# Up projection: half of the transposes of six column groups go from TensorE to SyncE's DMA queue, by way of two-byte planes

## The chip, the cores and the metric

The kernel runs on one core of a Trainium2 chip. The core has five engines with instruction streams of their own: TensorE (PE in the profile; PEld is its loading of weights), VectorE (DVE), ScalarE (ACT), GpSimd (POOL) and SyncE (SP). The data lie in SBUF, 128 partitions; products come out in PSUM; DMA queues, issued by SyncE, ScalarE and GpSimd, move data between SBUF and DRAM, and within SBUF.

The metric is the device time of one execution in microseconds, smaller is better. Before the change it was 1339.47 us, the median of three runs from 1339.23 to 1339.55. The profiled execution took 1339.37 us.

## What is computed

The reference is one encoder layer in float32: 256 tokens, width 2048. Two attention branches are gated, projected and added to the residual stream; then comes the part that the change touches, a squared-ReLU perceptron of inner width 8192:

```python
h = rms_norm(x, norm_mlp_pre[l])
u = jnp.square(jax.nn.relu(jnp.einsum('bsd,df->bsf', h, w_up[l])))
x = x + rms_norm(jnp.einsum('bsf,fd->bsd', u, w_down[l]), norm_mlp_post[l])
```

## The kernel before

Every product is made in split precision: each float32 operand is cut into a high part (a cast by ScalarE) and a low part (a subtraction on VectorE), and three products, high by high, high by low and low by high, are added in PSUM. Some blocks of a product are made with seven block products in place of eight. For those, VectorE makes sums of the weights (`u_0t`, `u_3t`, `u_5t`), which are split in turn (`u_0eh`, `u_0el` and so on).

The up projection has eight groups (`g` from 0 to 7), each of 1024 of the 8192 columns. A group has eight steps, one for each 256 rows of `w_up`; in most groups the order of the rows is 1, 2, 0, 4, 3, 6, 5, 7, and rows 0, 3 and 5 go by seven products. The raw weights of a step (1 MB) are loaded by SyncE into one of three buffers (`u_3r` is the raw tile of rows 3), and split into `u_3h` and `u_3l`. `Weights.next` (L710) asks for the weights of two steps ahead: at step `n` it traces the load and the split of position `n + 2`, each instruction of it ordered behind the instruction kept in `uw.behind` where the two are on the same engine. `u_piece` (L1183) adds the last partial result at the end of a group, sets `uw.behind` to that addition on VectorE, and lets ScalarE apply ReLU with the row's scale.

The result `z` of a group has tokens along the partitions: for each of two token blocks, two halves of 512 columns. The down projection needs it the other way around, so each half is transposed during the next group. `u_T` (L1165) does it: eight 128x128 transposes on TensorE (L1170) into two PSUM banks (`uT`), and a Square of each bank by ScalarE into a page `u` (L1173). It is called at the steps 1 and 2 of the group behind, for the first and the second half. `u_sets` then calls `act_sets`, which splits `u` into high and low parts (`ah`, `al`) and lets GpSimd store them in DRAM (`keeph`, `keepl`); for the first half, of even number, it also makes the sums `sm`. That happens at steps 3 and 5. The last group transposes both of its predecessor's halves at steps 1 and 2 and stores at 1 and 2, and the last group's own halves are transposed in the down projection.

A planner orders the instructions of each engine while the program is built: what is ready in its own model of time goes first, and among several, what was written first. On the chip each engine then runs its list in order, and SyncE starts its DMAs in order too. The pages of 4 KB a partition come from one pool of 27.

Of the kernel before, what the change touches and what calls it, by code (L numbers as in the profile page):

```python
# [10 lines left out]

F32 = mybir.dt.float32
F32R = mybir.dt.float32r
AF = mybir.ActivationFunctionType
ALU = mybir.AluOpType
AX = mybir.AxisListType

P = 128
D = 2048
T = 256  # L20
KD = D // P
DFF = 4 * D
# [28 lines left out]
def encoder_layer(ctx: ExitStack, tc: tile.TileContext, a, out):  # L51
    nc = tc.nc
# [12 lines left out]
    def page(shape, dt, name):  # L65
        return pages.tile(shape, dt, tag="pg", name=name)
# [4 lines left out]
    def t2k(name, dt=F32):  # L71
        return tmp.tile([P, 2, T], dt, tag="t2k", name=name, bufs=7)
# [6 lines left out]
    def small(w, name):  # L79
        return tiny.tile([P, w], F32, tag=f"s{w}", name=name)  # L80
# [37 lines left out]
    def split(raw, name, pieces=2, after=(), then=None):  # L118
# [3 lines left out]
        _, nk, cw = (P, len(raw), 512) if listed else raw.shape  # L122
        hi = wp.tile([P, nk, cw], F32R, tag="hi", name=f"{name}_h")
        lo = wp.tile([P, nk, cw], F32R, tag="lo", name=f"{name}_l")
        prev = front if then else ()
# [172 lines left out]

    hT = [page([P, 2, 512], F32R, f"hT{i}") for i in range(8)]

    def x_part(k):
# [3 lines left out]
        g = g_pre[:, k : k + 1]  # L305
        i = nc.scalar.activation(d[:, :T], src, AF.Copy, scale=g).ins
        j = nc.vector.scalar_tensor_tensor(  # L307
# [30 lines left out]
    def x_squares(i):  # L338
        for t in range(2):
            j = junk512("jx0").rearrange("p a b -> p (a b)")  # L340
            nc.scalar.activation(
                j, xp[i][:, t], AF.Square, accum_out=ssx[:, t * 4 + i : t * 4 + i + 1]
            )
# [10 lines left out]
    def head_constants():  # L354
# [5 lines left out]
        le = small(2, "le")  # L360
        nc.scalar.activation(le, ls, AF.Exp)
        nc.vector.scalar_tensor_tensor(
# [55 lines left out]
    def parts(dst, at, src):  # L418
        hi, lo = dst
        nc.scalar.copy(hi[at], src)  # L420
        nc.vector.tensor_sub(lo[at], src, hi[at].bitcast(F32))
# [34 lines left out]
    def v_evac(dst):  # L456
        hi, lo = dst

        def evac(t, ps):
            r = rx[:, t : t + 1]  # L460
            nc.scalar.activation(hi[:, t], ps, AF.Copy, scale=r)
            nc.vector.scalar_tensor_tensor(
# [5 lines left out]
    def p_transposed(p, name):  # L468

        pt = bank(f"{name}_pt")  # L470
        for kt in range(2):
            for t in range(2):
# [4 lines left out]
                )  # L477
        r = [t2k(f"{name}_pT{i}", F32R) for i in range(2)]
        parts(r, slice(None), pt.rearrange("p (k q) -> p k q", k=2))
        return r  # L480

    def diff_head(h, qT, kT, v, hl, sc):
        p = t2k(f"dp{h}")
        for t in range(2):
# [19 lines left out]
            for c in range(2):  # L504
                nc.scalar.activation(
                    e[:, c],
                    s[:, c * T : (c + 1) * T],
                    AF.Exp,
                    bias=nbs[:, c : c + 1],
# [27 lines left out]
        for t in range(2):  # L537
            nc.scalar.activation(
                on[:, t], o[:, t * T : (t + 1) * T], AF.Square, accum_out=ss[:, t : t + 1]
            )  # L540
# [5 lines left out]
        for eb in range(2):  # L546
            for t in range(2):
# [4 lines left out]
                )  # L552
        ot = page([P, 2, 512], F32R, f"oaT{h}")
        for eb in range(2):
# [8 lines left out]
    def na_head(h, qT, kT, v, hl):  # L563
# [47 lines left out]
        if h % 2 == 0:  # L611
            oT["nt", h // 2] = page([P, 2, 512], F32R, f"onT{h}")
        ot = oT["nt", h // 2][:, h % 2]
# [49 lines left out]
    def pair_weights(view, name, seven, low=None, after=None, paged=False):  # L663
# [32 lines left out]
            nc.vector.tensor_sub(l2[i], t[i], h2[i].bitcast(F32))  # L696
        return h1, l1, h2, l2

    class Weights:


# [73 lines left out]
    def wide_group(name, kinds, weights, stat7, stat8, mm_banks, z, piece, each=None, turn=None, after={}, in_order=False):  # L775

        any7 = any(s for _, s in kinds)
        pr = Products(name, mm_banks)  # L780
        pr.in_order = in_order
        for n, (i, seven) in enumerate(kinds):
            w = weights.next(after)
            if each:
                each(n)
            if seven:
                final = not any(s for _, s in kinds[n + 1 :])
                pr.seven(partial(stat7, i), w, final)
                if final:
                    pr.combine(z)  # L790
                continue
            end = n == len(kinds) - 1
            if turn and n < 2:
                ahead = [*ahead, (i, w)] if n else [(i, w)]
                for t in range(2) if n else ():
                    for ii, ww in ahead:
                        for which in (2 * t, 2 * t + 1):
                            pr.eight(partial(stat8, ii), ww, which, False)
                    if not t:
                        turn()  # L800
                continue
            for which in range(4):
                pr.eight(partial(stat8, i), w, which, end)
                if end:
                    b, t, half = PLAIN[which]
                    piece(t, half, pr.ps[b], any7)

    def sums_of(p1, p2, name):

        a11, a21, a12, a22 = p1[:, :P], p1[:, P:], p2[:, :P], p2[:, P:]  # L810
        s = page([P, 4, P], F32, f"{name}s")
        nc.vector.tensor_sub(s[:, 0], a21, a22)
        nc.vector.tensor_sub(s[:, 1], a11, a21)
        nc.vector.tensor_sub(s[:, 2], s[:, 0], a11)
        nc.vector.tensor_add(s[:, 3], a12, s[:, 2])
        parts_ = page([P, 2, 4, P], F32R, name)
        nc.scalar.copy(parts_[:, 0], s)
        nc.vector.tensor_sub(parts_[:, 1], s, parts_[:, 0].bitcast(F32))
        return parts_
# [77 lines left out]
    for h in range(2):  # L897
        gate = []
        for br, gc, src, o in (("a", GA, a["w_branch_a"], "a"), ("b", GB, a["w_branch_b"], "n")):
            z = [page([P, 2, 512], F32, f"g{br}{h}{t}") for t in range(2)]  # L900
# [183 lines left out]
    def first_up(n):  # L1084
        for t, c in {2: [(1, 1), (0, 2)], 3: [(1, 2), (0, 3)], 4: [(1, 3)]}.get(n, ()):
            residual_parts(t, c)
        if n == 5:
            for t in range(2):
                mlp_squares(t)
                mlp_scale(t)  # L1090
            for i in range(4):
                kd = dram.tile([P, 1024], F32, name=f"keepx{i}", tag=f"keepx{i}")
                nc.gpsimd.dma_start(kd, x2[i])
                kept["x", i] = kd
# [67 lines left out]
    def u_T(cg, z):  # L1162

        u = page([P, 4, T], F32, f"u{cg}")
        for b in range(2):  # L1165
            pt = bank(f"uT{cg}{b}")
            for j in range(2):
                for t in range(2):
                    c = (b * 2 + j) * P
                    nc.tensor.transpose(  # L1170
                        pt[:, j * T + t * P : j * T + (t + 1) * P], z[t][:, cg % 2, c : c + P], ident
                    )
            nc.scalar.activation(  # L1173
                u[:, b * 2 : b * 2 + 2], pt.rearrange("p (j q) -> p j q", j=2), AF.Square
            )
        return u

    def u_sets(cg, u):

        got = act_sets(cg, u)  # L1180
        if NG - 4 <= cg < NG - 2:
            sets[0, cg] = got
# [11 lines left out]
    def ups(g):  # L1194
        return ALL8 if g == 0 else LAST_UPS if g == DFF // 1024 - 1 else UPS

    uw = Weights()
# [19 lines left out]
                uw.ask(wd[:, :, cg, j, g * 1024 : (g + 1) * 1024], f"d{g}{cg}{j}", seven, page)  # L1217
    uz = None
    us = {}
    for g in range(DFF // 1024):  # L1220
        z = Late(lambda g=g: [page([P, 2, 512], F32, f"u{g}{t}") for t in range(2)])

        def up_each(n, g=g, uz=uz):
            if not g:
                first_up(n)
                if n == 7:
                    for i in (0, 3, 5):
                        f = page([P, 2, T], F32, f"h2f{i}")
                        for k in range(2):
                            d = hT2[i][:, k].bitcast(F32)  # L1230
                            nc.vector.tensor_add(f[:, k], d[:, :T], d[:, T:])
                        h2sum[i] = sums_of(f[:, 0], f[:, 1], f"h2s{i}")
                return
            cg = g * 2 - 3 + n
            if n in (1, 2):
                us[cg] = u_T(cg, uz)
            steps = (3, 5) if g < DFF // 1024 - 1 else (1, 2)
            if n in steps:
                cg = g * 2 - 2 + steps.index(n)
                u_sets(cg, us[cg])  # L1240

        wide_group(
            f"u{g}",
            ups(g),
            uw,
            h2stat7,
            h2stat8,
            (1, 2, 3, 7),
            z,
            partial(u_piece, z=z),  # L1250
            each=up_each,
            turn=None if g else turn_rows,
            after={} if g else {2: scaled[0]},
        )
        uz = z
# [133 lines left out]
    for g in range(2):  # L1389
        pr = Products(f"p{g}", (1, 2, 3, 7))  # L1390
        pr.in_order = True
        for bi, b in enumerate(blocks[g]):
            end = bi == len(blocks[g]) - 1
            for n, (cg, j, seven) in enumerate(down_steps(g, bi)):
# [42 lines left out]
                for which in range(4):  # L1437
# [4 lines left out]
                    if last:  # L1442
                        bank_, t, half = PLAIN[which]
# [65 lines left out]
```

## Time and profile before

| | us |
|---|---|
| median of three runs | 1339.47 |
| the profiled execution, its own time | 1339.37 |
| its span in the profile | 1337.6 |
| ScalarE busy | 740.3 |
| one up group, from start to start | 43.3 |
| transposes of the up projection, in number (16 blocks of 8) | 128 |

The span is the time from the first to the last instruction on the core; the execution's own time is a little longer. A row of a group of instructions names the line, the engine, the operation, what is written and read, and its count and time. A row of the timeline begins with its start in us from the start of the span and its length; in brackets stands the idle time of the engine before it and what ended it. A matmul's length covers its whole passage through the array, so neighbours overlap; the distance of the starts is what one costs. In a list of waits the engine that waits stands first, then what it waited for, the sum, the number and the longest.

### The profile page before, as it was taken

What the parts mean: (1) busy time and instruction counts of PE and PEld (TensorE: products, weight loads), DVE (VectorE), ACT (ScalarE), POOL (GpSimd) and SP (SyncE); (2) the same over time, 40 slices, a digit from 0 to 9 for tenths busy, and PEclk for the clock granted to TensorE, in tenths of its full rate; (3) what the DMA queues carried; (4) which work ended last, traced back from release to release, by engine and by line L of the source; (5) the groups of instructions that cost most, each with busy time, mean ns of one, the idle gap of its engine ahead of it and who ended that gap; (6) DMA issues with size and microseconds to landing.
All of it is one profiled execution on the core that took longest, in us unless ns stands there. A gap on an engine that the chain in (4) does not pass through costs nothing.

```text
span 1337.6 us, 16286 instructions
## 1 busy us (share of the span) xinstructions
PE 1329.0 (99%) x6305; PEld 1113.4 (83%) x6305; DVE 1096.8 (82%) x1277; ACT 740.3 (55%) x869; POOL 39.4 (3%) x73
## 2 busy tenths in 40 slices
PE   9999999999999999999999999999999999999997
PEld 8888888888888888888888888888888888888886
DVE  7978766667787897885688999999988988898886
ACT  6655554544545555555476666666555555555542
POOL 0000000000000000000100000000000000000000
PEclk9999999999999999999999999999999999999999
DMA  9874655564564656567658677877797998798995
GB/s 354 277 215 161 193 168 176 184 187 157 189 220 172 207 190 207 188 232 254 226 184 277 239 253 273 297 239 245 250 360 287 402 379 311 271 372 330 358 351 207
DMA packets 114125, 335.85 MB, mean 251 GB/s; under 512 B 16768, under 2 KB 17280, under 8 KB 114048
## 3 DMA queue, kind: packets, MB, share of 16 engines
q1 hardware_dynamic: 94368, 265.87, 57.5%
q10 hardware_dynamic: 12960, 43.26, 8.4%
q0 software_dynamic: 6720, 25.69, 4.9%
q8 instruction: 49, 0.80, 0.2%
q14 instruction: 28, 0.23, 0.0%
HBM read 307.01 MB, written 29.61 MB: 252 GB/s over the span
## 4 chain that ended last, share of the span: by engine, by line
PE 75%; issue 21%; DMA 1%; DVE 1%; ACT 1%; POOL 0%; SPq 0%; POOLq 0%; ACTq 0%
PE u L742 25%; PE ga L742 6%; PE gb L742 6%; PE ba L742 3%; PE bb L742 3%; PE y L742 3%; PE qn_p L223 2%; PE ka_p L223 2%; PE kn_p L223 2%; PE qa_p L223 2%; PE ka_p L225 1%; PE qn_p L225 1%; PE kn_p L225 1%; PE vn_p L267 1%; PE vn_p L266 1%
## 5 line engine op out<-in xcount | busy, mean ns | idle before, releaser
L223 PE MATMUL qn_p<-hT,qn_h 128*128 128x512 f32 x128 | 45.9, 400 | 0.0
L223 PE MATMUL kn_p<-hT,kn_h 128*128 128x512 f32 x128 | 45.6, 400 | 0.0
L223 PE MATMUL ka_p<-hT,ka_h 128*128 128x512 f32 x128 | 45.2, 399 | 0.0
L742 PE MATMUL u<-u_2h,h2T 128*128 128x512 f32 x128 | 44.0, 396 | 0.0
L223 PE MATMUL qa_p<-hT,qa_h 128*128 128x512 f32 x128 | 43.6, 399 | 0.3 <-DVE hT L307 0.3
L742 PE MATMUL u<-u_1h,h2T 128*128 128x512 f32 x128 | 43.4, 389 | 0.0
L742 PE MATMUL u<-u_4h,h2T 128*128 128x512 f32 x128 | 43.2, 391 | 0.0
L742 PE MATMUL u<-u_7h,h2T 128*128 128x512 f32 x128 | 41.0, 389 | 0.0
L742 PE MATMUL u<-u_6h,h2T 128*128 128x512 f32 x128 | 41.0, 389 | 0.0
L225 PE MATMUL qn_p<-hT,qn_l 128*128 128x256 f32 x128 | 35.9, 281 | 0.0
L225 PE MATMUL kn_p<-hT,kn_l 128*128 128x256 f32 x128 | 35.7, 280 | 0.0
L225 PE MATMUL ka_p<-hT,ka_l 128*128 128x256 f32 x128 | 35.2, 282 | 0.0
L225 PE MATMUL qa_p<-hT,qa_l 128*128 128x256 f32 x128 | 32.5, 282 | 0.1
L145 DVE TENSOR_TENSOR y_l<-y_w,y_h 128x1024 fp32r<-128x1024 f32 x16 | 19.0, 1222 | 11.9 <-ACT y_h L137 11.9
L223 PEld LDWEIGHTS kn_p<-hT,kn_h 128*128 128x128 f32 x128 | 24.0, 188 | 5.4
L223 PEld LDWEIGHTS qn_p<-hT,qn_h 128*128 128x128 f32 x128 | 24.1, 188 | 5.3
L145 DVE TENSOR_TENSOR kn_l<-kn_w,kn_h 128x1024 fp32r<-128x1024 f32 x16 | 19.0, 1220 | 11.5 <-ACT kn_h L137 11.5
L223 PEld LDWEIGHTS ka_p<-hT,ka_h 128*128 128x128 f32 x128 | 23.9, 188 | 5.3
L742 PEld LDWEIGHTS u<-u_1h,h2T 128*128 128x128 f32 x128 | 24.0, 188 | 5.0
L145 DVE TENSOR_TENSOR vn_l<-vn_w,vn_h 128x1024 fp32r<-128x1024 f32 x16 | 19.0, 1221 | 11.2 <-ACT vn_h L137 11.2
L742 PEld LDWEIGHTS u<-u_7h,h2T 128*128 128x128 f32 x128 | 24.0, 188 | 5.0
L742 PEld LDWEIGHTS u<-u_6h,h2T 128*128 128x128 f32 x128 | 24.0, 188 | 5.0
(1632 smaller groups left out, 4567.5 us busy)
## 6 DMA issues: line engine op xcount, KB each, us to landing
bh<-keeph ACTq DMA_DIRECT2D x30, 512.0 KB, 9.1
bl<-keepl ACTq DMA_DIRECT2D x30, 512.0 KB, 10.6
keeph<-ah POOLq DMA_DIRECT2D x18, 512.0 KB, 3.8
keepl<-al POOLq DMA_DIRECT2D x18, 512.0 KB, 7.1
va_w<-in_w_in SPq DMA_DIRECT2D x8, 1024.0 KB, 5.2
qn_w<-in_w_in SPq DMA_DIRECT2D x8, 1024.0 KB, 5.2
kn_w<-in_w_in SPq DMA_DIRECT2D x8, 1024.0 KB, 5.1
vn_w<-in_w_in SPq DMA_DIRECT2D x8, 1024.0 KB, 5.0
```

Of the source, the lines that this page charges most:

```text
L145: sub = nc.vector.tensor_sub(lo[part], src, hi[part].bitcast(F32)).ins
L223: nc.tensor.matmul(ps[b], hi[:, k % 4, cs], mv, start=(k == 0), stop=False)
L225: nc.tensor.matmul(ps[b][:, :T], lo[:, k % 4, cs], mv[:, :T], start=False, stop=(k == nk - 1))
L266: nc.tensor.matmul(ps[t], sh, hi[:, k % 4], start=(k == 0), stop=False)
L267: nc.tensor.matmul(ps[t], sh, lo[:, k % 4], start=False, stop=False)
L742: ins = nc.tensor.matmul(self.ps[i], st, mv[:, blk], start=i not in self.begun, stop=last and n == 2).ins
```

## The change

For the groups 1 to 6 (`by_dma`), the second half of the previous group's columns no longer goes through `u_T`. At step 1, ahead of the first half's `u_T`, `sent` splits each float32 into its two 16-bit halves: ScalarE copies, for each token block, 512 numbers a partition, read as 1024 two-byte elements at a stride, into two planes (low and high halves). One DMA from SyncE's queue then transposes the 128 x 2048 two-byte elements into a page `got`, 16 blocks of 128 x 128. At step 3, `joined` lets ScalarE copy the 2048 elements a partition back, interleaved, into a page `u`, and a Square over the whole page follows in place. The storing at steps 3 and 5 stays. `uw.behind` is set to the transposing DMA, so the loads that are traced from step 2 of the group on, those of position 4 and after, follow it in SyncE's queue. Group 7 and the down projection keep TensorE's transposes for both halves.

```diff
+    def sent(z, name):
+
+        planes = page([P, 2, 2, 512], U16, f"{name}_s")
+        for t in range(2):
+            nc.scalar.copy(planes[:, t], z[t].bitcast(U16).rearrange("p (c h) -> p h c", h=2))
+        got = page([P, 16, P], U16, f"{name}_g")
+        moved = nc.sync.dma_start(got, planes.rearrange("p t h c -> p (t h c)"), transpose=True)
+        return got, moved.ins
+
+    def joined(got, dst):
+
+        nc.scalar.copy(
+            dst.rearrange("p k q -> p (k q)")
+            .bitcast(U16)
+            .rearrange("p (k t q h) -> p t h k q", k=4, t=2, h=2),
+            got.rearrange("p (t h k) q -> p t h k q", t=2, h=2),
+        )
...
             cg = g * 2 - 3 + n
-            if n in (1, 2):
+            by_dma = g < DFF // 1024 - 1
+            if n == 1 and by_dma:
+                uh[cg + 1], uw.behind = sent([uz[t][:, 1] for t in range(2)], f"u{cg + 1}")
+            if n == 1 or n == 2 and not by_dma:
                 us[cg] = u_T(cg, uz)
-            steps = (3, 5) if g < DFF // 1024 - 1 else (1, 2)
+            if n == 3 and by_dma:
+                cg = g * 2 - 1
+                us[cg] = page([P, 4, T], F32, f"u{cg}")
+                joined(uh[cg], us[cg])
+                nc.scalar.activation(us[cg], us[cg], AF.Square)
+            steps = (3, 5) if by_dma else (1, 2)
```

More of the change, by code (lines that the diff above doesn't have):

```diff
@@ L13 @@
 F32R = mybir.dt.float32r
+U16 = mybir.dt.uint16
 AF = mybir.ActivationFunctionType
@@ L1219, in encoder_layer @@
     us = {}
+    uh = {}
     for g in range(DFF // 1024):
```

## The prediction

> **What bounds the kernel now.** I read the page first, then the busy times in stretches of one up group each, then the chain of waits through one group. The group chosen, the one that begins at 780.5, is typical: the stretches repeat every 43.3 us.
>
> ```profile
> span 1337.6 us, 16286 instructions
> PE 1329.0 (99%) x6305; PEld 1113.4 (83%) x6305; DVE 1096.8 (82%) x1277; ACT 740.3 (55%) x869; POOL 39.4 (3%) x73
> 780.50:823.80 43.30, 43.30 (x201) 36.03 (x200) 40.02 (x41) 27.40 (x27) 3.24 (x6) 1.00 0.76 261
> 823.80:867.00 43.20, 43.20 (x201) 35.94 (x200) 39.93 (x40) 27.40 (x27) 3.24 (x6) 1.00 0.76 260
> L1170 PE MATMUL uT<-ident,u x128: 270/272/327, 696.5 to 1010.2; 128*128 128x128 f32 x128
> by line: PE u L742 96.4%; PE uT L1170 4.0%
> 789.24 0.88 PE uT L1170 x8
> 790.11 2.74 PE u L742 x12
> 792.85 0.87 PE uT L1170 x8
> ```
>
> The columns of the stretches are length, then busy time and count of PE, PEld, DVE, ACT and POOL, clock, DMA share and GB/s. TensorE is busy through the whole group at clock 1.00, and the chain inside it has nothing but PE: matmuls of L742 and two blocks of eight transposes (L1170), 0.88 and 0.87 us each. VectorE is second with 40.02 of 43.30 us. So time taken off PE is time gained, until VectorE, 3.3 us behind, becomes the bound.
>
> **What the change takes off.** One block of eight transposes in each of six groups: 6 x 0.88 = 5.3 us, that is 0.40%. The two evictions of that block (Square, L1173, 0.6 us each) also go from ScalarE. Nothing else of PE's work changes: the matmuls behind the block simply move up.
>
> **What it adds on ScalarE.** Three things per group: two copies of 128x1024 two-byte elements (planes), one copy of 128x2048 (the join), one Square of 128x1024.
>
> ```profile
> 782.09 2.56 ACT L1188 ACTIVATE u<-u,r 128x512 f32<-128x512 f32 x4
> 784.55 1.03 ACT L695 CAST u_0eh<-u_0t 128x1024 fp32r<-128x1024 f32 x1
> 788.16 1.05 ACT L695 CAST u_0eh<-u_0t 128x1024 fp32r<-128x1024 f32 x1 [2.58 <-DVE u_0t L685]
> 789.32 1.91 ACT L677 CAST u_4h<-u_4r 128x2048 fp32r<-128x2048 f32 x1
> 791.13 1.08 ACT L1173 ACTIVATE u<-uT 128x512 f32<-128x512 f32 x2
> ...
> 793.03 1.50 ACT L682 CAST u_3h<-u_3r 128x1536 fp32r<-128x1536 f32 x1
> ```
>
> No row has a strided two-byte copy. The nearest are the casts of as many elements, 1.05 us for 1024 and 1.91 for 2048. If time goes by bytes they halve, and if a 2-byte stride costs a second pass they double: 0.5 to 2.1 and 1.0 to 3.8 us. I take the cast rows, as they have the element counts. ScalarE then has 27.4 - 1.1 + 2 x 1.05 + 1.9 + 1.05 = 31.4 us in a group of 42.4 (37 at the upper ends): it stays under the others, and its idle time hides the sum. The place matters more. The rectified rows are complete at 784.65; the next cast runs to 785.6, and then ScalarE idles 2.58 us. The two plane copies fit into that gap: 785.6 to 787.7. The following casts start as before.
>
> **What it moves: SyncE's queue.** The transposing DMA waits for the second plane copy, and SyncE is in order. The change also sets `uw.behind` to this DMA after the load of position 3 of the group has been asked for. The first load behind it is therefore position 4, u_3r, and then u_6r.
>
> ```profile
> 778.10 0.37 SPq L667 DMA_DIRECT2D u_3r<-in_w_up  x1
> 788.19 0.37 SPq L667 DMA_DIRECT2D u_6r<-in_w_up  x1
> u_3r<-in_w_up SPq DMA_DIRECT2D x2, 1024.0 KB, 8.0
> u_6r<-in_w_up SPq DMA_DIRECT2D x2, 1024.0 KB, 5.0
> L383 SPq DMA_DIRECT2D bias<-skew x16: 585/626/1400, 140.9 to 284.2; - x16
> DMA to landing us min/median/max: 2.8/4.6/5.5
> keeph<-ah POOLq DMA_DIRECT2D x4, 512.0 KB, 3.6
> DMA  9992100068950389768998999449998999799999
> ```
>
> (The last line is the DMA engines' busy tenths in forty slices of the group, 1.08 us each, from 780.0: they stand nearly idle from 783.2 to 788.7.) u_3r leaves at 778.10 today; it would leave after 787.7 plus the time for which the transposing DMA holds SyncE and the queue. That hold is the unknown of this case, as no transposing DMA is in the trace. Lower end: 0.37 us, the issue of a plain load (128 partitions x 2 rows = 256 runs of 4 KB). The bias load has 64 partitions x 6 = 384 runs of 256 B and takes 0.60 us: 128 more runs, 0.23 us more, 1.8 ns a run. Cut into 256-byte runs (one output row of 128 two-byte elements) the 512 KB are 2048 runs: 0.37 + 1792 x 1.8 ns = 3.6 us. Cut into 32-byte runs (16 elements) they are 16,384: 29 us, the upper end. I take **3.6 us**, since 256 bytes is both the row of the bias and the row of the output. The data itself is small: 512 KB land 3.6 us after issue in the keep row.
>
> [...]
>
> **What is late next.** With 3.6 us u_3r leaves at 787.7 + 3.6 = 791.3, 13 us later than now, and with the 5.0 us of u_6r (its neighbour, which also starts on idle DMA engines) it lands at 796.3.
>
> ```profile
> 789.24 1.22 DVE L696 TENSOR_TENSOR u_0el<-u_0t,u_0eh 128x1024 fp32r<-128x1024 f32 x1 [1.12 <-ACT u_0eh L695]
> 790.39 1.22 DVE L683 TENSOR_TENSOR u_3t<-u_3r 128x1024 f32<-128x1024 f32 x1
> 791.52 2.28 DVE L679 TENSOR_TENSOR u_4l<-u_4r,u_4h 128x2048 fp32r<-128x2048 f32 x1
> 793.72 0.69 DVE L684 TENSOR_TENSOR u_3t<-u_3t,u_3r 128x512 f32<-128x512 f32 x1
> ...
> 795.46 1.75 DVE L686 TENSOR_TENSOR u_3l<-u_3r,u_3h 128x1536 fp32r<-128x1536 f32 x1
> ...
> 801.84 0.42 DVE L1113 TENSOR_TENSOR sm<-u 128x256 f32<-128x256 f32 x1
> ...
> 808.63 1.22 DVE L1129 TENSOR_TENSOR al<-sm,ah 128x1024 fp32r<-128x1024 f32 x1
> ```
>
> ```profile
> 802.64 0.39 PE L742 MATMUL u<-u_3l,h2s 128*128 128x512 f32 x1
> ...
> 804.23 0.39 PE L742 MATMUL u<-u_3el,h2s 128*128 128x512 f32 x1
> ```
>
> ```profile
> DVE u_1l L679 <- ACT u_1h L677: 0.9, 1, 0.9
> DVE u_6l L679 <- ACT u_6h L677: 0.7, 1, 0.7
> DVE u_7l L679 <- ACT u_7h L677: 0.4, 1, 0.4
> 815.59 1.04 ACT L1128 CAST ah<-u 128x1024 fp32r<-128x1024 f32 x1
> ```
>
> The first of these fences is VectorE in order of time, the second PE, the third VectorE's waits in the same group and the cast that takes the columns in question.
>
> PE first needs all of u_3 at 802.64 - 0.88 = 801.8, and its sums (u_3el) at 803.3. From a landing at 796.3: u_3h by a cast of 1.5 us (797.8), u_3l 1.75 (799.6), then the two remaining short adds of 0.69 and u_3el 1.22: 802.2. So PE does not wait, with about 1.1 us in hand. VectorE, which today takes up u_3t at 790.39, can first do u_4l from 791.2 (2.28) and the work on the preceding columns, four sums of 0.42 and al<-sm of 1.22, 2.9 us that is ready from 792.2: filled until 796.4, apart from 0.8 us before u_4l. It may idle 42.4 - 40.0 = 2.4 us a group, so this is covered. If the order on VectorE is not so changed, it waits 796.3 - 793.5 + 0.8 = 3.6 us at this place, 1.2 more than it has: that cover gone costs 1.2 a group, more than the gain.
>
> So the price has an edge: a hold up to about 4.7 us costs nothing, 5.6 us eats the 0.88, and each microsecond beyond costs 6 us in all. The join is no such edge. Its data precede u_3r in the same queue, and its result is used by the odd columns' cast, which today runs at 815.6; only if it is placed ahead of u_3h on ScalarE does it push that by 1.9 + 1.05 us, against the 1.1 us in hand. I cost it at zero, hidden by the 20 us in between. Pages of SBUF: the planes and their transpose take two, but u's page comes two steps later and the two of z go back after the first block: about even, cost zero.
>
> **The sum.** 0 on ScalarE, 0 on VectorE, -5.3 on PE. The profiled execution took 1339.37 us with a span of 1337.6; the 1.8 around it stays. It lies 0.1 under the median of the runs, so the forecast is 1339.5 - 5.3 = **1334.2 us**.
>
> **The rivals.** First, *slower: SyncE is held.* The transposing DMA is issued or drained in small pieces, so that u_3r, u_6r behind it arrive after PE has run out of u_4. It decides from a hold of 5.6 us; 7 us gives 6 x 1.4 = +8 (1348), 10 us gives +26 (1366), the 29 us of the upper bound +140. For it: 1.8 ns a run is a slope from two rows, and the queue is in order. Against: the DMA engines idle while u_3r would be late, so nothing else slows it. [...]
>
> Second, *no change: VectorE becomes the bound.* It waits for u_3r in its old order and loses 0.5 to 1.3 us per group, so the gain becomes -2.5 to +2.5: 1337 to 1342. For it: 40.0 of 42.4 leaves little. Against: three of its four waits today (0.7, 0.4 and 0.9 us, for casts that wait for PE) vanish when it runs late. Chance 0.20.
>
> **How the numbers follow.** A measurement of this kernel tells about 0.2%, 2.7 us, from no change. Forecast 0.48 (1333.5 to 1336.7), no change 0.20, slower 0.32, and the three chances are these. The lower end of the range is the whole PE gain and 0.7 us of drift in the other stages, 1333.5; the upper end takes in a hold of 7.6 us, 1352, and leaves out longer holds, about 0.16.
>
> **What would show it.** Right: the transposes of the up projection (uT) number 80 in place of 128, the group's period is 42.4 us with PE busy throughout, u_3r leaves under 5 us after the transposing DMA, and no wait of PE for u_3h, u_3l or u_3el appears. Wrong: PE idle before u_3 or u_6 with u_3r as the last cause; VectorE waiting more than 2.4 us a group; the plane copies not in the gap at 785.6 but behind u_4h, which would make u_3r 3.5 us later still; ScalarE held at the join.

## The result: 1385.1 us, 3.4% slower

| | before | after |
|---|---|---|
| median of the runs, us | 1339.51 | 1385.10 |
| ratio, with its 95% interval | | 1.0338 (1.0326 to 1.0351) |
| the profiled execution's span, us | 1337.6 | 1382.6 |
| one up group, us | 43.3 | 51.2 |

The forecast was 1334.2, with a range from 1333.5 to 1352. The change costs 45.6 us, and it costs them in the six groups that it touches. The page of the kernel after, and its busy times in one group (length, then busy time and count of PE, PEld, DVE, ACT and POOL, clock, DMA share, GB/s):

```profile
span 1382.6 us, 16185 instructions
PE 1344.4 (97%) x6257; PEld 1115.5 (81%) x6257; DVE 1096.2 (79%) x1277; ACT 764.8 (55%) x881; POOL 39.3 (3%) x73
```

```profile
804.80:856.00 51.20, 46.02 (x193) 36.51 (x192) 40.78 (x40) 31.52 (x30) 3.23 (x6) 0.93 0.66 231
```

PE has 48 matrix instructions fewer, as meant, and yet is busy for longer. Its group splits into three parts. Without the block of transposes it needs 43.30 - 0.88 = 42.4 us. It idles 51.20 - 46.02 = 5.2 us. In the remaining 46.02 - 42.4 = 3.6 us its matmuls take longer. By an estimate from the starts in the timeline some 2 us of that are ten matmuls that start 0.41 to 0.59 us apart in place of 0.23, at a lower clock (0.93 in the mean of the group). Most of the rest, some 0.9 us, lies ahead of the four stops: there a matmul counts with the whole length of its row, 0.39 to 0.63 us, where one with a follower counts 0.23. Together that is 7.9 us more than before, and six such groups are 47 us, about what was measured.

In this group the lower clock comes behind idle time. Stretches of 4 us near its end:

```profile
834.00:838.00 4.00, 1.40 (x5) 0.87 (x6) 1.83 (x3) 3.10 (x3) 0.00 (x0) 0.93 0.94 329
838.00:842.00 4.00, 2.70 (x6) 1.70 (x7) 3.76 (x4) 1.17 (x2) 0.84 (x2) 0.50 0.90 363
842.00:846.00 4.00, 4.00 (x14) 3.15 (x14) 3.96 (x8) 1.93 (x2) 0.22 (x1) 0.71 0.35 143
```

PE is busy 1.40 of 4 us, then the granted clock is 0.50 for a while and comes back some 4 us after PE is fed again without a break (840.3 to 844.3). This split says where PE's time went, and not that the clock makes the group longer: VectorE, whose additions end the group, has only 0.24 us of idle time ahead of its combining operations there (841.63). By that, most of what a full clock would have saved PE would have become idle time; no run tests it. What PE waits for, and what VectorE waits for ahead of it, from the list of waits over the six groups (sum, number, longest):

```profile
DVE u_3t L684 <- DMA u_3r<-in_w_up: 37.0, 6, 7.2
...
ACT u_2h L678 <- DMA u_2r<-in_w_up: 20.6, 6, 3.7
...
PE u L761 <- DVE u_5el L697: 14.5, 11, 1.8
...
PE u L761 <- ACT u_5eh L696: 13.0, 6, 2.5
```

VectorE waits 6 us in each group for the load of rows 3, and PE pays for it later, at rows 5. There ScalarE adds to it: in the group shown it has the cast of the next group's rows 2 ahead of the second `u_5eh`, and waits 3.69 us for that load first. SyncE's queue in that group, and the transposing DMA over all six groups:

```profile
784.06 0.37 SPq L668 DMA_DIRECT2D u_4r<-in_w_up  x1
805.54 1.33 SPq L706 DMA_TRANSPOSE u_g<-u_s  x1
807.28 0.38 SPq L668 DMA_DIRECT2D u_3r<-in_w_up  x1
807.76 0.45 SPq L668 DMA_DIRECT2D u_6r<-in_w_up  x1
808.31 0.41 SPq L668 DMA_DIRECT2D u_5r<-in_w_up  x1
```

```profile
L706 SPq DMA_TRANSPOSE u_g<-u_s x6: 1329/1598/1732, 703.3 to 958.8; - x6
...
DMA to landing us min/median/max: 3.6/3.7/3.9
```

Between 784.1 and 805.5 SyncE starts nothing. Then the transposing DMA leaves, and behind it, without a pause, come three loads. Counted from the end of ReLU they leave 15.9, 6.3 and 1.2 us later than before the change. With three raw buffers, that of u_6r was free from the last use of u_0's (800.7). The DMA itself is quick: 1.6 us to issue and 3.7 us to land. It is late because its planes are late. ScalarE in order of time:

```profile
797.23 0.72 ACT L1207 ACTIVATE u<-u,r 128x512 f32<-128x512 f32 x1
800.77 1.05 ACT L696 CAST u_0eh<-u_0t 128x1024 fp32r<-128x1024 f32 x1 [2.82 <-DVE u_0t L686]
801.73 1.04 ACT L704 COPY u_s<-u 128x1024 uint16<-128x1024 uint16 x1
802.67 1.90 ACT L678 CAST u_4h<-u_4r 128x2048 fp32r<-128x2048 f32 x1
804.48 1.04 ACT L704 COPY u_s<-u 128x1024 uint16<-128x1024 uint16 x1
```

The rectified rows are complete at 797.95. The gap of 2.82 us that follows stays empty, and the second plane copy comes behind u_4h. VectorE in the same stretch:

```profile
804.61 2.29 DVE L680 TENSOR_TENSOR u_4l<-u_4r,u_4h 128x2048 fp32r<-128x2048 f32 x1 [1.53 <-ACT u_4h L678]
812.79 1.22 DVE L684 TENSOR_TENSOR u_3t<-u_3r 128x1024 f32<-128x1024 f32 x1 [5.89 <-DMA u_3r<-in_w_up]
```

It does nothing in the 5.89 us, and from 812.8 to the additions that end the group (846.6) it has only 2.4 us of idle time left. This closes a ring. The additions and ReLU end `z`; `z` lets the plane copies run; they release the DMA; the loads stand behind it; VectorE needs the loads for the work that ends at the next group's additions. From ReLU to ReLU (797.95 to 848.12) the ring takes 50.2 us, of which 14.8 go by before u_3r has landed. Before the change u_3r left 6.5 us ahead of the end of ReLU, so the load did not hang on it.

### The profile page after: what moved, and what is told of

It is laid out like the page before. It is cut to its first block, busy times and chain, and to the rows that moved or that the text cites. A ratio compares the mean times of both kernels' runs of the same rounds, so it can differ in the third digit from the quotient of the medians.

```text
span 1382.6 us, 16185 instructions
## 1 busy us (share of the span) xinstructions
PE 1344.4 (97%) x6257; PEld 1115.5 (81%) x6257; DVE 1096.2 (79%) x1277; ACT 764.8 (55%) x881; POOL 39.3 (3%) x73
## 5 line engine op out<-in xcount | busy, mean ns | idle before, releaser
L761 PE MATMUL u<-u_7h,h2T 128*128 128x512 f32 x128 | 46.1, 425 | 0.0
L224 PE MATMUL kn_p<-hT,kn_h 128*128 128x512 f32 x128 | 45.6, 400 | 0.0
L1207 ACT ACTIVATE u<-u,r 128x512 f32<-128x512 f32 x32 | 21.4, 712 | 32.4 <-DVE u L1206 27.9
L684 DVE TENSOR_TENSOR u_3t<-u_3r 128x1024 f32<-128x1024 f32 x7 | 8.6, 1224 | 37.0 <-DMA u_3r<-in_w_up 37.0
L761 PEld LDWEIGHTS u<-u_7h,h2T 128*128 128x128 f32 x128 | 27.4, 214 | 6.3
L683 ACT CAST u_3h<-u_3r 128x1536 fp32r<-128x1536 f32 x7 | 10.4, 1484 | 36.5 <-DMA u_3r<-in_w_up 36.5
L680 DVE TENSOR_TENSOR u_2l<-u_2r,u_2h 128x2048 fp32r<-128x2048 f32 x8 | 18.3, 2290 | 14.5 <-ACT u_2h L678 14.5
L680 DVE TENSOR_TENSOR u_4l<-u_4r,u_4h 128x2048 fp32r<-128x2048 f32 x8 | 18.3, 2292 | 14.0 <-ACT u_4h L678 14.0
L761 PE MATMUL u<-u_5eh,h2s 128*128 128x512 f32 x36 | 16.3, 481 | 13.0 <-ACT u_5eh L696 13.0
```

The lines of the kernel that those rows point to most:

```text
L224: nc.tensor.matmul(ps[b], hi[:, k % 4, cs], mv, start=(k == 0), stop=False)
L680: nc.vector.tensor_sub(l1, raw, h1.bitcast(F32))
L683: nc.scalar.copy(h1[:, 1:4], raw[:, 1:4])
L684: nc.vector.tensor_add(t[0], raw[:, 1:3], raw[:, 0:1].to_broadcast([P, 2, 512]))
L761: ins = nc.tensor.matmul(self.ps[i], st, mv[:, blk], start=i not in self.begun, stop=last and n == 2).ins
L1207: nc.scalar.activation(zt, zt if summed else ps, AF.Relu, scale=r2[:, t : t + 1])
```

## The experiments

Three theories stood at the start. Q: the loads' place behind a DMA that waits for the preceding group is what costs. A: ScalarE's added work and its order cost. T: the transposing DMA itself holds the queue or disturbs what runs beside it. All ratios are against runs of the kernel before on the same chip, with 95% intervals. Every edit lets the planner order the engines anew, so a difference between two runs can hold more than the edit.

**Loads no longer behind the DMA (e1_loads_free).**

```diff
-                uh[cg + 1], uw.behind = sent([uz[t][:, 1] for t in range(2)], f"u{cg + 1}")
+                uh[cg + 1], _ = sent([uz[t][:, 1] for t in range(2)], f"u{cg + 1}")
```

> The kernel after, but the loads are no longer ordered behind the transposing DMA (uw.behind stays what u_piece set). Theory Q (queue): the 7.9 us lost per group come from the three loads u_3r, u_6r, u_5r, which wait behind a DMA that waits for the end of the preceding group; freed, the loads leave ahead of it and the group falls to 42.4 to 43.3 us: 1334 to 1340 in all, u_3r leaving at or before the plane copies. Theory A (ScalarE): the copies and the join, 4 us more of ScalarE per group, and where they stand in its order delay the casts; then the order of the loads matters little: 1370 to 1386. If the planner still puts the loads behind the DMA by itself, nothing changes and the two are not told apart.

1341.14 us, ratio 1.0014 (1.0004 to 1.0023): 44 of the 45.6 us are gone with one assignment. The transposing, the copies and the join are all still there, so theory A falls as the cause of the 45.6 us. ScalarE, SyncE and a group of this kernel, and PE's wait in all six:

```profile
781.01 2.78 ACT L1207 ACTIVATE u<-u,r 128x512 f32<-128x512 f32 x4
...
790.93 1.99 ACT L704 COPY u_s<-u 128x1024 uint16<-128x1024 uint16 x2
```

```profile
776.99 0.37 SPq L668 DMA_DIRECT2D u_3r<-in_w_up  x1
788.20 0.37 SPq L668 DMA_DIRECT2D u_6r<-in_w_up  x1
792.94 1.66 SPq L706 DMA_TRANSPOSE u_g<-u_s  x1
```

```profile
749.75:792.94 43.19, 42.67 (x193) 35.10 (x192) 40.07 (x40) 31.37 (x30) 3.23 (x6) 1.00 0.82 274
```

```profile
PE u L761 <- DVE u L1206: 3.8, 6, 1.2
```

u_3r leaves 16 us ahead of the DMA, and the clock is 1.00 again. The copies are no earlier here than in the kernel after: the DMA leaves 9.1 us after the end of ReLU (783.79), in place of 7.6. So their late place costs little by itself; it costs where the loads stand behind it. But the group is 43.2 us, not 42.4: the gain of 5.3 us is missing, the time is 1.1 us above theory Q's range, and a wait of PE for VectorE's additions at the turn of the group has appeared. The runs from e5 on, but for e8, are about that.

**A small DMA in place of the transposing one (e3_small_dma).** TensorE transposes as before; the wait and the order are kept.

```diff
-        moved = nc.sync.dma_start(got, planes.rearrange("p t h c -> p (t h c)"), transpose=True)
+        kz = dram.tile([16, 2, 16], U16, name=f"{name}_k", tag=f"{name}_k")
+        moved = nc.sync.dma_start(kz, planes[:16, :, 0, :16])
...
-            if n == 1 or n == 2 and not by_dma:
+            if n in (1, 2):
                 us[cg] = u_T(cg, uz)
-            if n == 3 and by_dma:
...
```

> TensorE transposes both halves as before the change, and there is no transposing DMA and no join; the plane copies stay, and in place of the transposing DMA stands a plain one of 1 KB that reads the planes, with the loads ordered behind it. The planes are not used for the result. Theory Q: the wait is what costs, not the transposing: 1370 to 1392. Theory A: only the copies are left of the added 4 us, so less than half of the loss stays: 1340 to 1360. A theory T, that the transposing DMA itself holds the queue or slows what runs beside it: 1339 to 1343.

1379.8 us in its one time, 40 above before. The same ring with a DMA of 1 KB, a group and VectorE's wait in all six:

```profile
805.30:856.70 51.40, 46.30 (x203) 36.39 (x202) 38.96 (x40) 29.30 (x30) 3.23 (x6) 0.97 0.63 220
```

```profile
DVE u_3t L684 <- DMA u_3r<-in_w_up: 33.1, 6, 6.5
```

Theory T falls: without any transposing DMA the loss is nearly whole. Theory Q holds.

**The DMA from ScalarE's queue (e2_scalar_queue).** e1's edit, and:

```diff
-        moved = nc.sync.dma_start(got, planes.rearrange("p t h c -> p (t h c)"), transpose=True)
+        moved = nc.scalar.dma_start(got, planes.rearrange("p t h c -> p (t h c)"), transpose=True)
```

> As in the run before, and the transposing DMA is issued from ScalarE's queue, so SyncE's queue holds only loads and cannot be held by it at all. Theory Q: 1334 to 1340, a group of 42.4 to 43.3 us. Theory A: as slow as the kernel after or slower (1375 to 1395), as 1.6 us of issue per group comes on top on ScalarE.

1358.27 us, ratio 1.014 (1.0125 to 1.0155), between the two expectations. SyncE is free here, so the 17 us above e1 come with the move of the issue to ScalarE:

```profile
798.86 2.35 ACTq L706 DMA_TRANSPOSE u_g<-u_s  x1
801.25 1.09 ACT L1192 ACTIVATE u<-uT 128x512 f32<-128x512 f32 x2 [1.05 <-issue]
```

ScalarE's next instruction starts where the row of the issue ends (801.2), 1.05 us after ScalarE was free. VectorE waits for ScalarE's casts, 3.9 us in four groups for u_3h, for which it does not wait in three groups of e1. That this makes all of the 17 us was not shown; the planner also orders ScalarE differently here.

**The copies early (e4_copies_early), and early with the loads free (e8_early_and_free).** In `u_piece`, behind the ReLU of the second block's half:

```diff
+        if (t, half) == (1, 1) and g < DFF // 1024 - 2:
+            early[g] = sent([z[s][:, 1] for s in range(2)], f"u{g * 2 + 1}")
...
-                uh[cg + 1], uw.behind = sent([uz[t][:, 1] for t in range(2)], f"u{cg + 1}")
+                uh[cg + 1], uw.behind = early[g - 1]
```

> The kernel after, with the plane copies and the DMA written earlier, in u_piece right behind the ReLU of the second token block's half, so that they come ahead of the next group's casts on ScalarE; the loads stay behind the DMA. Theory Q: the DMA leaves some 5 to 6 us earlier in the group, u_3r lands about 9 us after the ReLU instead of 15, which is before VectorE needs it: most of the loss goes, 1335 to 1348. Theory A: the copies take the same time and push the casts of rows 0 and 4 later instead: 1370 to 1390.

> Plane copies early as in e4_copies_early and the loads free as in e1_loads_free. e4_copies_early kept 14 us of the loss. Theory Q: that rest is still u_3r behind the DMA, so free loads take it away: 1336 to 1342. Theory P (place): the early copies stand between ReLU and the next casts and make VectorE and PE late by themselves: 1347 to 1354.

e4 gave 1353.35 in one time, e8 1346.21, ratio 1.0047 (1.0034 to 1.0061). Neither expectation is met in full. Moving the copies takes 32 of the 45.6 us away, freeing the loads then another 7, but e8 stays 5 above e1. The early copies seem to cost something by their place; no run tells that from the planner's new order. PE's wait for the additions, first in e4, then in e8:

```profile
PE u L761 <- DVE u L1208: 13.9, 6, 3.5
```

```profile
PE u L761 <- DVE u L1208: 5.7, 6, 3.1
```

**Is VectorE's amount of work the new bound? (e5_less_vector, e6_before_less_vector, e7_low_on_gpsimd)** In `act_sets`, for the odd column groups 1 to 11:

```diff
+            odd = cg % 2 == 1 and cg < NG - 4
+            lo = hi if odd else page(shape, F32R, f"al{cg}{i}")
...
-                nc.vector.tensor_sub(lo[:, at], src, hi[:, at].bitcast(F32))
+                if not odd:
+                    nc.vector.tensor_sub(lo[:, at], src, hi[:, at].bitcast(F32))
```

e5 has this on e1, e6 on the kernel before; in e7, also on e1, nothing is left out and these subtractions go to `nc.gpsimd.tensor_sub`.

> Freed loads as in e1_loads_free, and the low part of the odd column groups 1 to 11 isn't made (the high part is stored in its place): 1.22 us less of VectorE per group. e1_loads_free came out 7 us above the forecast of this change, with PE waiting 0.5 to 1.2 us per group for the additions of VectorE (L1206). Theory V: VectorE's chain at the end of the group has taken the place of the transposes as the bound; with 1.22 us less of it the 0.88 us per group appear: 1333 to 1337. Theory A: ScalarE's 4 us more per group and its order hold the group at 43.2; VectorE's work is no matter: 1340 to 1342.

> The kernel before with the same low parts left out, as a control. Theory V: PE alone bounds the group there, so 1.22 us less of VectorE gain nothing: 1338.5 to 1340. If it gains as much as e5_less_vector does over e1_loads_free, VectorE was the bound before as well and theory V does not tell the two apart.

> Freed loads, and the low parts of the odd column groups 1 to 11 are made by GpSimd in place of VectorE, so nothing is left out. Theory V: as e5_less_vector, 1333 to 1337, below both kernels, if GpSimd's subtraction does not slow VectorE. If GpSimd and VectorE disturb each other, VectorE's subtractions next to it take visibly longer than their 1.22 and 2.29 us, and it is 1338 to 1346. Theory A: 1340 to 1342.

1340.56, ratio 1.0007 (0.9998 to 1.0016); 1339.55, ratio 1.0002 (0.9992 to 1.0011); 1340.26, ratio 1.0004 (0.9995 to 1.0012). Theory V as I put it is wrong: 1.22 us less of VectorE per group, taken alone, changes hardly anything. VectorE's timeline in e5 at the turn of a group shows why; the second fence is PE in e5, the third PE in the kernel before:

```profile
817.86 2.29 DVE L680 TENSOR_TENSOR u_2l<-u_2r,u_2h 128x2048 fp32r<-128x2048 f32 x1
821.02 0.69 DVE L789 TENSOR_TENSOR u<-u,u 128x512 f32<-128x512 f32 x1 [0.88 <-PE u L761]
821.75 0.69 DVE L790 TENSOR_TENSOR u<-u,u 128x512 f32<-128x512 f32 x1
822.35 0.68 DVE L1209 TENSOR_TENSOR u<-u,u 128x512 f32<-128x512 f32 x1
```

```profile
820.98 0.39 PE L761 MATMUL u<-u_5eh,h2T 128*128 128x512 f32 x1
...
823.09 0.50 PE L761 MATMUL u<-u_1h,h2T 128*128 128x512 f32 x1 [0.36 <-DVE u L1209]
```

```profile
777.06 0.39 PE L742 MATMUL u<-u_5eh,h2T 128*128 128x512 f32 x1
...
780.46 0.39 PE L742 MATMUL u<-u_1h,h2T 128*128 128x512 f32 x1
```

VectorE now waits for PE, for the last products of rows 5, and only then can do the two operations that combine the seven products and the first addition, 2.0 us, for which the next group's first product waits. In the kernel before, the last product of rows 5 starts 3.4 us ahead of the next group's first (777.06 and 780.46), and the chain fits. In e5 the planner has put it later: 2.1 us ahead, with the wait of 0.36 us in it.

**The order at the turn (e9_turn_order, e10_turn_and_gpsimd, e11_products_first, e12_products_first_no_gpsimd).** Two edits: the split of the next group's first rows is ordered behind the last split of rows 5 (e9, and with e7's GpSimd e10), and TensorE does the products of rows 5 in written order, with those of rows 7 behind them (e11 on top of e10, e12 on top of e9).

```diff
+            with ExitStack() as order:
+                for ins in ends if turn(name) else ():
+                    order.enter_context(tc.issue_after(ins))
+                nc.scalar.copy(h1, raw)
...
+                if final and name in [f"u{g}" for g in range(1, DFF // 1024 - 1)]:
+                    pr.in_order = True
                 pr.seven(partial(stat7, i), w, final)
```

> Freed loads as in e1_loads_free, and the split of the next group's first rows (u_1h, u_1l) is ordered behind the last split of rows 5 (u_5eh, u_5el) on ScalarE and VectorE, the order that the kernel before has by itself. Theory O (order at the turn): with u_1 ahead, u_5el comes late, TensorE does the last products of rows 5 about 1.5 us before the group's end in place of 3.2, and VectorE's chain of two combining operations and the first addition (2.0 us) no longer fits in, so TensorE waits 0.4 to 1.2 us. With the order back the wait goes: 1334 to 1337, a group of 42.4 to 42.7 us. Theory A (ScalarE's added work): 1340 to 1342 as before. Theory V is dropped: 1.22 us less of VectorE changed nothing that can be told from zero.

> As e9_turn_order, with the low parts of the odd column groups on GpSimd as in e7_low_on_gpsimd. If theory O holds and VectorE is near its limit in a group of 42.4 us (40.1 of it busy), the 1.22 us less leave nothing more to wait for: 1334 to 1336, equal to or a little under e9_turn_order. If e9_turn_order alone reaches 1334.5, this one is the same.

> As e10_turn_and_gpsimd, and in groups 1 to 6 TensorE does the products of rows 5 in written order and those of rows 7 behind them, so the three VectorE operations of the turn have the 24 products of rows 7 (5.4 us) to run beside. In e10_turn_and_gpsimd the split of rows 5 was in time (u_5el ready at 816.3), but TensorE's planned order put its last products 1.2 us before the group's end, and VectorE's chain of 2.0 us did not fit. Theory O in its second form (the planned order of the products at the turn): the wait for the additions goes, a group of 42.4 to 42.6 us, 1333.5 to 1336.5. Theory A (ScalarE's added copies hold the group): 1339.5 to 1342.

> The same without GpSimd: all low parts on VectorE, the split order of e9_turn_order and the product order of e11_products_first. Theory O: if VectorE's 40.1 us in 42.4 suffice, 1334 to 1337.5; if it takes both the order and the 1.22 us, 1338 to 1342 here against 1333.5 to 1336.5 there, which makes VectorE's share of the turn a condition of its own.

e9: 1343.03, ratio 1.0026 (1.0016 to 1.0036). e10: 1341.12, 1.0012 (1.0003 to 1.0021). e11: 1338.43, 0.9991 (0.9982 to 1.0001). e12: 1340.38, 1.0003 (0.9995 to 1.0012). The order of the split is a miss, both without GpSimd (e9) and with it (e10). The order of the products with 1.22 us off VectorE (e11) gives the forecast group for the first time, though its time lies between its two expectations; without the 1.22 us (e12) nothing is gained. A group of e11:

```profile
795.19:837.61 42.42, 42.42 (x193) 35.22 (x192) 39.06 (x39) 31.35 (x30) 7.16 (x7) 1.00 0.80 279
```

That is 43.30 - 0.88; three more of its groups took 42.37 to 42.38. Its first group did not do so. GpSimd, VectorE and PE there:

```profile
730.65 3.55 POOL L1161 TENSOR_TENSOR al<-u,ah 128x1024 fp32r<-128x1024 f32 x1 [8.78 <-ACT ah L1160]
```

```profile
732.41 3.94 DVE L688 TENSOR_TENSOR u_2l<-u_2r,u_2h 128x2048 fp32r<-128x2048 f32 x1 [0.47 <-ACT u_2h L686]
```

```profile
738.41 0.65 PE L771 MATMUL u<-u_1h,h2T 128*128 128x512 f32 x1 [1.87 <-DVE u L1219]
```

Behind GpSimd's subtraction VectorE's took 3.94 us in place of 2.29 (the last section has the rows of both), PE idled 1.87 us, and its matmuls then started 0.43 us apart in place of 0.23, until 742.4; the granted clock from 740 to 752 was 0.92.

**The rest (e13_order_and_left_out, e14_gpsimd_five, e15_control_before).** e13 is e12 with e5's parts left out; e14 is e11 with GpSimd in five groups only; e15 has e14's edits on the kernel before, without the change.

```diff
-            low = nc.gpsimd if cg % 2 == 1 and cg < NG - 4 else nc.vector
+            low = nc.gpsimd if cg in (3, 5, 7, 9, 11) else nc.vector
```

> The order of e12_products_first_no_gpsimd, with the low parts of the odd column groups 1 to 11 left out (the high part is stored in their place), so neither VectorE nor GpSimd makes them. Theory O with VectorE's share: without the stall that GpSimd brought into the first group of e11_products_first, all six groups stand at 42.4 us and the term of -5.3 us appears whole: 1333.5 to 1336. If something else of the change still costs (ScalarE, the transposing DMA beside the loads), 1337 to 1341.

> As e11_products_first, with GpSimd making the low parts of the odd column groups 3 to 11 only; group 1's stays on VectorE. If the 1.9 us wait and the slower clock behind it in e11_products_first's first group came from GpSimd's subtraction beside VectorE's (3.94 us for a 2.29), they go: 1334 to 1337. If VectorE is then late in the first group by its own 1.22 us, or GpSimd disturbs another group, 1337 to 1340.

> The control to e14_gpsimd_five: the kernel before, with TensorE's transposes for both halves, and the same three edits (split order, product order, GpSimd for five low parts), without the change. If e14_gpsimd_five gains by the transposes taken off TensorE, this one stands where the kernel before stands, 1338.5 to 1341, as TensorE has nothing to wait for there. If the edits gain by themselves, it is at 1336 to 1338 too and the change has no part in it.

e13: 1336.72, ratio 0.9979 (0.9970 to 0.9988), 0.7 us above its expectation. With e1 this makes a square: neither edit 1341.14 (e1), less work of VectorE 1340.56 (e5), the order alone 1340.38 (e12), both 1336.72. So it takes both.

e14: 1336.83, ratio 0.9980 (0.9971 to 0.9989), as expected. That is below both kernels, 0.2% below the kernel before, with nothing left out. e15: 1344.25, ratio 1.0035 (1.0021 to 1.0048), which misses its expectation: the same edits without the change cost 4.6 us. They gain nothing there, but e15 is no clean control. GpSimd and VectorE in one of its groups:

```profile
817.71 3.56 POOL L1142 TENSOR_TENSOR al<-u,ah 128x1024 fp32r<-128x1024 f32 x1 [6.03 <-ACT ah L1141]
```

```profile
819.47 3.95 DVE L687 TENSOR_TENSOR u_2l<-u_2r,u_2h 128x2048 fp32r<-128x2048 f32 x1 [0.47 <-ACT u_2h L685]
```

GpSimd's subtraction starts ahead of `u_2l` in all five groups of e15, and `u_2l` takes 3.94 to 3.95 us. In e14 VectorE starts first in all five, and `u_2l` keeps its 2.28 to 2.29. The starts of GpSimd's subtractions lie 44.1 us apart in e15, 0.8 more than a group before; five times that is 4.2 us, most of what e15 loses. That e14 gains by the transposes is read from the groups instead. In the kernel before PE has 201 matrix instructions a group, is busy for all of 43.30 us and waits for nothing, so there is no wait that a new order could take away. In a group of e14 it is busy throughout too, with 193:

```profile
792.74:835.10 42.36, 42.36 (x193) 35.16 (x192) 39.04 (x39) 31.30 (x30) 7.16 (x7) 1.00 0.80 280
```

PE's waits in the up projection, first e14's, then e15's:

```profile
PE u L771 <- DVE u L1219: 0.8, 1, 0.8
```

```profile
PE u L752 <- DVE u L1200: 3.0, 5, 0.6
```

e14 gains 2.8 us where the term is 5.3. Its load `d000r` for the down projection leaves at 996.17 against 999.76, so 3.6 us are won by then; group 1 still loses about 1 us, and one execution's span ends 2.6 us ahead. Where the last microsecond goes was not followed.

## Why the prediction was wrong, step by step

**The term of -5.3 us on PE was right in size.** A group without the block takes 42.4 us in e11 and e14. It appears only if the loads are free, the turn of the group keeps its order and VectorE has 1.22 us less to do. The step "time taken off PE is time gained" missed the last two: by e12 VectorE's 40 us in a group of 42.4 were not enough, though they fit as a sum.

**ScalarE's durations were near**: the plane copies take 1.04 us (1.05 taken), the Square 1.06 (1.05), the join 2.52 (1.9 taken, 3.8 the upper end). The upper ends add up to 36.4 us a group, not 37.

**The hold of the queue was over-sized, and the wrong thing to ask for.** I took 3.6 us, from a slope of 1.8 ns a run (the median of the bias row, 0.63 us in place of 0.60, would have made it 2.0 ns and 4.0 us). The issue takes 1.3 to 1.7 us, with a median of 1.6, and u_3r follows 1.7 us behind. That it goes by runs of 256 bytes, as I took it, was my estimate and no run shows it.

**The first step that failed is the place of the plane copies: "785.6 to 787.7", in the gap behind ReLU.** I read a gap in the profile as free for new work. But the order is fixed by the planner, and it put the copies behind the casts written ahead of them. So the DMA could leave 7.6 us after ReLU in place of 3.1, and u_3r landed 14.8 us after it in place of 11.7. Why the planner left the gap empty was not settled. The prediction named this as what would make it wrong, "3.5 us later still", but gave it no chance and no price. By itself this step does not explain the loss: in e1 the DMA leaves still later after ReLU, 9.1 us, and 44 of the 45.6 us are gone.

**The second, which decides, is the price of a late u_3r.** By my own edge (12.8 us after ReLU, and 6 us in all for each microsecond beyond) the late landing would have cost 12 us, against a gain of 5.3: 1346, still inside the range. It cost 51. I had counted on VectorE filling the wait with the sums of the preceding columns ("filled until 796.4"); it did u_4l and then waited instead, 5.89 us. PE itself waits only 0.7 us in all for u_3l, in two of the six groups, so that part of the reckoning held. But I had priced one pass, where the end of each group releases the next group's loads, so that VectorE's lateness returns as the DMA's lateness: the ring takes 50.2 us where a group took 43.3. e1 takes the loads out of the ring and nothing else in the source, e3 leaves the ring and takes the transposing out, and the loss goes with the first and stays with the second. I had no term for the clock either; that it has a part in the loss is not shown.

**The rivals.** "Slower: SyncE is held" named the queue and the sign, but its mechanism was a slow issue, with PE out of work behind u_4. What held SyncE was the wait for data, and PE stood at rows 5. "VectorE becomes the bound" was right in that its wait shows first, at rows 3, and that with the loads free the turn of the group goes by VectorE's chain. There both the chain's place and the amount of work count, as e5, e12 and e13 show.

## What to carry to other kernels

Before a DMA that waits for an engine goes into a queue of prefetches, ask what stands behind it and by how much that used to run ahead: here it was not the DMA's cost but the 16 us of lead that u_3r lost, and one assignment brought back 44 of 45.6 us. If the waiting DMA depends on the end of the stage that its followers feed, the loss can repeat in every round: the transposing DMAs of the six groups started 51.1 us apart in the mean, where a group had taken 43.3. And an idle gap in a profile is not a place for new work unless the order that fills it is known.

## What the runs showed of the hardware that was not expected

One stall of some 2 us was followed by slow matmuls, and two others were not. In e11 one idle time of 1.87 us was followed by about 4 us with starts 0.43 us apart (738.4 to 742.4); in e10 one of 1.86 us at the same place (738.63) was not, nor was one of 2.34 us in e9 (825.72): the matmuls behind them started 0.23 us apart again after the first one or two. The granted clock from 690 to 1000 was 0.99 in e11 and 1.00 in e10 and e9.

A DMA that transposes 128 x 2048 two-byte elements within SBUF lands in 3.6 to 3.9 us from SyncE's queue in the kernel after and in 3.7 to 4.2 us in e1; the 1 MB loads of the group shown took 4.9 to 9.4 us. From ScalarE's queue it took 4.1 to 7.5 us, with a median of 7.2 (e2); in the group shown u_5r's load left 0.4 us behind it.

GpSimd's and VectorE's subtractions look as if they took turns in these traces. GpSimd's of 128x1024 takes 3.55 to 4.12 us where VectorE's takes 1.22. But in all 28 cases of e7, e10, e11, e14 and e15 VectorE is at a subtraction of 128x2048 when GpSimd's starts, and GpSimd's ends 2.24 to 2.28 us after that one. In the seven cases in which `u_2l` starts while GpSimd is at work (one in e10, one in e11, five in e15) it takes 3.94 to 3.95 us and ends 2.14 to 2.15 us after GpSimd's; in the 21 in which it starts first it keeps its 2.28 to 2.29 us. So by these rows it is as if the one that starts second waited for the first, though no row has GpSimd's alone, and the subtractions moved to GpSimd cost VectorE's next one nothing only where VectorE started first.
